# Turning the keys of a gated-recurrence layer by DMA and ScalarE instead of by TensorE

## The chip, the cores and the metric

The kernel runs on one core of one Trainium2 chip. The metric is the device time of one execution in microseconds, the median over the runs shown. The engines are TensorE (PE, its weight loads PEld), VectorE (DVE), ScalarE (ACT), GpSimd (POOL), and SyncE (SP), whose queue issues nearly all transfers of this kernel. Each engine works through its own instructions in order.

## The reference, cut to what matters

One layer over 2048 latent tokens and 256 context tokens of width 1024: adaLN-modulated norm, one input projection to 9216 columns, two groups of heads, one output projection, gated residual, final norm. Eight heads of width 128 run a gated linear recurrence in both directions; a gated short convolution fills the other half.

```python
def chunk_scan(q, k, v, logf, s0):
    """S_t = diag(f_t) S_{t-1} + k_t v_t^T, o_t = S_t^T q_t, chunkwise."""
    def step(S, inp):
        qc, kc, vc, gc = inp
        bcum = jnp.cumsum(gc, axis=2)
        ...
        o = einsum('bhts,bhsv->bhtv', attn, vc) + einsum('bhtk,bhkv->bhtv', qc * jnp.exp(bcum), S)
        S_new = jnp.exp(b_last)[..., None] * S + einsum(
            'bhsk,bhsv->bhkv', kc * jnp.exp(b_last[:, :, None, :] - bcum), vc)
        return S_new, o
...
q, i, zf, zb = [p_hg[..., j * HG_WIDTH:(j + 1) * HG_WIDTH] for j in range(4)]
f_f = lb_f + (1.0 - lb_f) * sigmoid(zf)      # k = 1 - f, logf = log(f); the same backward
o, _, _ = bidir_scan(q, kf, kb, v, gf, gb, s_f, s_b)     # s_f, s_b: states after the context
y_hg = hgrn_out(o, p[..., 4 * HG_WIDTH:HG_COLS], hg_onorm_w[l], x.dtype)
```

## The kernel before, in words

**Stretches.** The program is written as 50 stretches (`stretch`, from line 1255 on): 32 head stretches (head `a` of 8, i = 0 to 3, each one segment of 512 tokens), four of the first convolution block, 14 pairs, and then the output projection. A head runs its four segments forward if its number is even, backward if odd (`prim`). So the group of tokens changes at i = 1, 2 and 3, and stays the same from i = 3 to the next head's i = 0.

**Products.** A head stretch has two units (gates, then values and queries), a third one for the output gates at odd i, and at i = 0 three short ones for the context. A unit is the seven products of a Strassen-like scheme (`seven`, line 954), each 4 x 3 matmuls of 128x128 by 128x256 f16, as each operand is split into a high and a low half. ScalarE copies out the banks `p1`, `p5` and `u2` (`keep`, line 970) before the next product adds onto the same bank, and VectorE takes the four results (`plus`, line 974). The last product of a unit is issued after the first product of the next (`finish_unit`). The right-hand operands ("hop" tiles, nine, seven to a stretch) are loaded by SyncE at line 1423 as the last unit of the stretch before frees them.

**The order of the work.** Everything else is cut into steps with a weight (`PACE`, `paced`): `chain` (the scan) and `extra` (second passes, gates, w_out). `merge_steps` spreads each list over the stretch by its weights, and `run` issues a step when its share of the ticks is reached; a tick is three matmuls, 28 to a unit. What is left is issued at the end of the stretch. So a step's place in every engine's queue, SyncE's too, is written by hand through its weight. The weights of the scan's steps (the context's first step, `c_first`, has 1.5; `out2` 1.0, `rstd` 0.63):

```python
PACE = {
...
        "c_levels": 4.27, "c_keys": 0.85, "c_states": 0.31, "values": 0.65, "begin": 1.0, "levels": 1.55, "held": 1.1,
        "level6": 2.64, "keys": 1.0, "states": 2.0, "out": 0.53, "states2": 1.14,
...
```

**The scan of a segment** runs in the stretch after its own (`scan_steps`): the values are turned, then levels 0 to 6 multiply the keys K and queries Q by gate products (`levels`, `held`, `level6`, `update`; VectorE at L509, L516, L522, ScalarE's mixed copies at L626, TensorE's attention blocks A at L656, L675, L682 into the pool `pa`). The gates' products are written into a tile `tot` of their own. Then the keys are turned, then the chunk states are formed, then the output:

- `key_turn` (line 692): for each of the two directions four TensorE transposes of 128x128 f32 into a bank of `px` (L697), and one copy out by ScalarE (L699).
- `states`: four products T of turned keys and values per direction (`outer`, L706); VectorE steps the states of the head's own direction (L750); ScalarE keeps the other direction's T (`Ts`, L755).
- `outp`: eight products o (L762, L763) and a copy by ScalarE (L765).

**Segments with fast values.** From segment 7 on (`FAST = 7`, to segment 31) the values are turned without TensorE, by `Turn`: `over` reads the 128x512 f32 tile as 128x1024 two-byte words in one transposing DMA (L122), `back` brings the halves into place with four DMAs (L128), and `join` interleaves them into f32 by a ScalarE copy (L132). Segments 0 to 6 use `value_turn`: four TensorE transposes and a copy.

**Second passes.** When a head's four segments are done, the other direction runs over them (`second_steps`: VectorE steps states Z at L802, four products at L809, an addition at L810, four sums of squares by ScalarE at L812); then `head_rstd` (twelve small VectorE operations, L155 to L161) and `y_steps` (scaling by ScalarE at L858, four transposes at L864, VectorE at L866). All four second passes of a head and its rstd stand in the i = 1 stretch of the next head; `y_steps` follow in i = 2, i = 3 and i = 0.

**Buffers.** PSUM has eight banks: three for the products (`pm`), three in `pa`, two in `px` (turned values and keys, T, o, second passes, turned outputs, weight scales). The tag `pair` of the pool `hp` has four tiles of 2 KB a partition; it holds a transfer turn's two tiles, the early stores, and in heads 6 and 7 the rows of w_out that `wo_scan` loads and sums. K and f have two tiles each, Q six, the `ring` ten.

Of the kernel before, what the change touches and what calls it, by code (L numbers as in the profile page):

```python
# [33 lines left out]
FAST = 7  # L34
# [28 lines left out]
def hybrid_layer(ctx: ExitStack, tc, x, cx, w_ada, b_ada, w_in, w_out, fnorm_w, small_d, masks, ident_d, sel_d, out):  # L63
# [15 lines left out]
    pa = ctx.enter_context(tc.tile_pool(name="pa", bufs=3, space=PSUM))  # L79
    px = ctx.enter_context(tc.tile_pool(name="px", bufs=2, space=PSUM))  # L80
# [33 lines left out]
    class Turn:  # L114
# [5 lines left out]
        def over(s):  # L120
            s.a = hp.tile([P, 2 * NCH, P], U16, tag="pair", name=f"ta_{s.nm}", bufs=4)
            SY.dma_start_transpose(s.a, s.src().bitcast(U16))  # L122

        def back(s):
            s.b = hp.tile([P, NCH, 2, P], U16, tag="pair", name=f"tb_{s.nm}", bufs=4)
            for h in range(2):
                for b in range(2):
                    SY.dma_start(s.b[64 * b:64 * b + 64, :, h, :], s.a[h::2, b::2, :])  # L128
# [136 lines left out]
    def norm_group(ntile, src, row0, m, nm, first_ops=None, space=q_tile):  # L265
# [72 lines left out]
        def store2(ops, k, row, eng):  # L338

            n2 = len(ops)  # L340
            pair = hp.tile([P, n2, 2, HW], F16, tag="pair", name=f"hp{ops[0]}_{nm}{k}", bufs=4)
# [189 lines left out]
    class Seg:  # L531
# [208 lines left out]
    def scan_steps(h, s):  # L740
# [26 lines left out]
        turn_v = Turn(lambda: s.vT, f"v{s.nm}")  # L767

        def joined():
            s.v = turn_v.join()  # L770

        over, back, join = [], [], []
        if s.fast:
            over, back, join = [paced(0.2, turn_v.over)], [paced(0.2, turn_v.back)], [paced(0.6, joined)]
        return (over + ([] if s.fast else [paced("values", s.value_turn)]) + [paced("begin", s.begin_levels)]
                + [paced("levels", lambda: s.levels(0))] + back + [paced("held", lambda: s.held(1)),
                   paced("levels", lambda: s.levels(2)), paced("held", lambda: s.held(3))] + join
                + [paced("levels", lambda: s.levels(4))]
                + [paced("held", lambda: s.held(5)), paced("level6", s.level6), paced("keys", s.key_turn), paced("states", states),
                   paced("out", outp)])  # L780
# [266 lines left out]
    def wo_scan(k):  # L1047
        for j in range(2):
            half = hp.tile([P, GW], F32, tag="pair", name=f"wos{k}{j}", bufs=4)
            SY.dma_start(half, w_out[0, k * P:(k + 1) * P, j * GW:(j + 1) * GW])  # L1050
            S.activation(junk[:, :GW], half, AF.Abs, accum_out=late.rs[:, 2 * k + j:2 * k + j + 1])
# [179 lines left out]
    for hd in range(HEADS):  # L1231
# [29 lines left out]
    for wi, (kind, a, i) in enumerate(stretch):  # L1261
        units, chain, extra = [], [], []
        if kind == "head":
# [26 lines left out]
            if i == 1:  # L1290
                chain += context_steps(h)
# [7 lines left out]
        if wi > 0 and stretch[wi - 1][0] == "head":  # L1299
            _, pa_h, pi = stretch[wi - 1]  # L1300
            chain += scan_steps(heads[pa_h], heads[pa_h].segs[pi])
# [5 lines left out]
        if prev is not None:  # L1307
            if i == 1:
                for j in range(NG):
                    extra += second_steps(prev, j)  # L1310
# [4 lines left out]
            elif i == 2 and prev is tail:  # L1315
# [403 lines left out]
```

## Time and profile before

| | |
|---|---|
| median of three runs | 2147.5 us (2145.26 to 2148.08) |
| profiled execution | 2148.78 us, span 2147.0 us |
| TensorE busy | 2065.5 us (96%) |
| VectorE busy | 1648.6 us (77%) |
| ScalarE busy | 1203.0 us (56%) |
| GpSimd busy | 193.8 us (9%) |
| DMA queue q1, share of 16 engines | 47.0% |
| granted TensorE clock | 0.994 |

The span is from the first to the last instruction of the profiled execution; the time of an execution is somewhat longer than its span. Busy time is the union of an engine's instructions. TensorE's matmuls overlap: a matmul's duration is its latency, and what it occupies is the distance to the next one's start. In a row of the timeline the columns are start, duration, engine, line, operation, output and inputs, and count; rows with "q" behind the engine are its sequencer's or its DMA issues. A tile's row gives the shortest, median and longest duration in ns and the first and last start in us. A row of waits gives the waiting instruction, whom it waited for, total us, times and the longest.

### The profile page before, as it was taken

How to read it: one execution, taken by the hardware profiler on the slowest of the kernel's cores; microseconds unless marked ns; L12 is line 12 of the kernel's file. 1: busy time of each engine (PE TensorE's matmuls, PEld its weight loads, DVE VectorE, ACT ScalarE, POOL GpSimd, SP SyncE). 2: the span in 40 equal slices, each digit the busy share in tenths (PEclk: the TensorE clock that was granted, in tenths of full speed). 3: DMA queues.
4: the chain of work that ended last, by engine and by line, in shares of the span. 5: the costliest groups of instructions: out<-in, count | busy, mean ns of one | idle time of the engine just before them, and what ended most of it. 6: DMA issues, size and time to landing. Idle time of an engine off the chain costs nothing. (4 is left out here: it accounts for less than half of the span.)

```text
span 2147.0 us, 53020 instructions
## 1 busy us (share of the span) xinstructions
PE 2065.5 (96%) x22011; PEld 1455.3 (68%) x22011; DVE 1648.6 (77%) x3413; ACT 1203.0 (56%) x2406; POOL 193.8 (9%) x272
## 2 busy tenths in 40 slices
PE   5988999999999999999999999999999999999998
PEld 2877878888888888888888887444444444444443
DVE  6787988878778787788787877687778655687775
ACT  7965666767567666676776655345444423333332
POOL 0121111111111111111111100000000000000000
PEclk8999999999999999999999999999999999999999
DMA  9567533452445343544654568833443105542421
GB/s 357 192 209 265 180 120 128 146 173 86 135 137 159 116 133 119 180 114 153 193 168 131 152 198 254 255 125 101 138 138 99 62 28 189 198 144 89 136 80 59
DMA packets 239398, 324.12 MB, mean 151 GB/s; under 512 B 66611, under 2 KB 168371, under 8 KB 237365
## 3 DMA queue, kind: packets, MB, share of 16 engines
q1 hardware_dynamic: 236996, 316.80, 47.0%
q8 instruction: 172, 2.82, 0.5%
q10 hardware_dynamic: 2160, 3.93, 0.5%
q14 instruction: 70, 0.57, 0.1%
HBM read 240.19 MB, written 67.37 MB: 143 GB/s over the span
## 5 line engine op out<-in xcount | busy, mean ns | idle before, releaser
L964 PEld LDWEIGHTS <-e_p 128*128 128x128 f16 x1332 | 130.4, 98 | 68.7 <-issue 19.0
L509 DVE TENSOR_TENSOR K<-K,tot 128x512 f32<-128x512 f32 x192 | 135.6, 706 | 42.8 <-ACT km L626 25.9
L626 ACT ACTIVATE km<-K 128x512 f32<-128x512 f32 x192 | 129.2, 674 | 69.7 <-DVE K L509 65.5
L963 PEld LDWEIGHTS <-e_p 128*128 128x128 f16 x1332 | 130.4, 98 | 53.2 <-issue 1.4
L965 PEld LDWEIGHTS <-e_p 128*128 128x128 f16 x1332 | 130.4, 98 | 52.0 <-issue 0.9
L516 DVE TENSOR_TENSOR Q<-Q,tot 128x512 f32<-128x512 f32 x192 | 132.9, 692 | 26.5 <-PE A L656 15.1
L633 POOL COPY qm<-Q 128x512 f32<-128x512 f32 x96 | 80.7, 840 | 781.6 <-DVE Q L516 781.6
L964 PEld LDWEIGHTS <-whib_p 128*128 128x128 f16 x888 | 87.0, 98 | 38.6 <-issue 5.2
L963 PEld LDWEIGHTS <-whib_p 128*128 128x128 f16 x888 | 86.9, 98 | 37.2 <-issue 0.8
L963 PEld LDWEIGHTS <-whia_p 128*128 128x128 f16 x888 | 86.9, 98 | 35.9 <-DMA hop3B<-Hd3B 2.4
L965 PEld LDWEIGHTS <-wloa_p 128*128 128x128 f16 x888 | 86.8, 98 | 35.1 <-issue 1.3
L965 PEld LDWEIGHTS <-wlob_p 128*128 128x128 f16 x888 | 86.9, 98 | 34.4
L964 PEld LDWEIGHTS <-whia_p 128*128 128x128 f16 x888 | 86.9, 98 | 33.4 <-issue 1.3
L181 ACT ACTIVATE e_p<-ws_p,sc_p 128x512 f16<-128x512 f32 x108 | 77.2, 718 | 56.9 <-DVE ws_p L468 40.0
L690 POOL COPY A<-Ac 32x128 f32<-32x128 f32 x128 | 79.5, 621 | 132.9 <-ACT A L686 103.8
L886 ACT ACTIVATE cv<-c,small 128x512 f32<-128x512 f32 (+1 forms) x36 | 24.3, 674 | 112.5 <-DVE c L904 63.3
L970 ACT ACTIVATE u<-sa,sx_w 128x256 f32<-128x256 f32 (+1 forms) x111 | 58.1, 523 | 47.0 <-PE sa L965 38.2
L1630 POOL TENSOR_TENSOR x_o<-x_o,fw 128x512 f32<-128x512 f32 x1 | 1.3, 1266 | 871.0 <-ACT junk L1621 871.0
L182 DVE SCALAR_TENSOR_TENSOR e_p<-ws_p,sc_p,e_p 128x512 f16<-128x512 f32 x108 | 79.4, 747 | 0.0
L433 ACT ACTIVATE junk<-ws_p 128x1024 f16<-128x1024 f32 x72 | 75.6, 1050 | 5.1 <-DMA ws_p<-in_w_in 4.9
L181 ACT ACTIVATE hiS_o<-y_o,sc_y 128x1024 f16<-128x1024 f32 x32 | 36.7, 1148 | 72.9 <-PE sa_o L964 32.1
L970 ACT ACTIVATE p<-sa,sx_w 128x256 f32<-128x256 f32 (+1 forms) x111 | 57.4, 517 | 24.1 <-PE sa L965 24.1
(863 smaller groups left out, 7044.8 us busy)
## 6 DMA issues: line engine op xcount, KB each, us to landing
ws_p<-in_w_in SPq DMA_DIRECT2D x72, 512.0 KB, 4.4
y_o<-yT SPq DMA_DIRECT2D x32, 512.0 KB, 4.2
xt_x<-in_x SPq DMA_DIRECT2D x16, 512.0 KB, 6.0
wa<-in_w_ada SPq DMA_DIRECT2D x16, 512.0 KB, 10.1
Gd<-zs SPq DMA_DIRECT2D x32, 256.0 KB, 2.9
sg<-Gd SPq DMA_DIRECT2D x32, 256.0 KB, 3.7
yT<-y SPq DMA_DIRECT2D x32, 256.0 KB, 2.4
wos<-in_w_out SPq DMA_DIRECT2D x32, 256.0 KB, 3.3
```

Source lines behind the costliest of these rows:

```text
L181: S.activation(hi, src, AF.Copy, scale=st[:, 0:1])
L182: V.scalar_tensor_tensor(lo, src, st[:, 0:1], hi, ALU.mult, ALU.subtract)
L433: S.activation(junk.rearrange("p (k n) -> p k n", k=KT), stage[i], AF.Abs, accum_out=r)
L509: V.tensor_tensor(m, m, sub(cur, nb + 1, [[2, np_], [-(nb + 1), 2], [0, B]]), ALU.mult)
L516: V.tensor_tensor(m, m, sub(cur, 1, [[2, np_], [nb - 1, 2], [0, B]]), ALU.mult)
L626: S.activation(sub(s.km, 0, [[2 * B, n // (2 * B)], [B, 2], [1, B]]), mix(s.K, n, B, n // (2 * B)), AF.Copy)
L633: G.tensor_copy(sub(qm, 0, [[2 * B, n // (2 * B)], [B, 2], [1, B]]), mix(s.qf, n, B, n // (2 * B)))
L690: G.tensor_copy(A3[js, :, js], s.Ac[js])
L963: PE.matmul(ps, hi[:, k], rh, start=start and k == 0, stop=False, skip_group_check=not start)
L964: PE.matmul(ps, hi[:, k], right(name, 1, k), start=False, stop=False, skip_group_check=not start)
L965: PE.matmul(ps, lo[:, k], rh, start=False, stop=k == nk - 1, skip_group_check=not start)
L970: last_keep.append(S.activation(r, ps, AF.Copy, scale=sx))
```

## The change

For segments 7 to 30 (`FAST = (7, 31)`), the keys too go through `Turn`, one turn for each direction. Segment 31 goes back to the TensorE turn for values, and keeps it for the keys. The steps of two segments now share a stretch (`scan_chain`): the new segment's levels, and the old segment's key joins, states and output, which are so issued about half a stretch later than before. The keys' transfers are the last step of the chain. The totals are written over the gates (`s.tot = s.f`). `pa` goes from three banks to two, `px` from two to three, the tag `pair` from four tiles to six. For heads whose last segment is fast, two of the second passes stay in the next head's i = 1 stretch, behind a pause of weight 8, and the other two and the rstd go to i = 2. `wo_scan` is split into a step that fetches and a step that sums.

```diff
-FAST = 7
+FAST = (7, 31)
-    pa = ctx.enter_context(tc.tile_pool(name="pa", bufs=3, space=PSUM))
-    px = ctx.enter_context(tc.tile_pool(name="px", bufs=2, space=PSUM))
+    pa = ctx.enter_context(tc.tile_pool(name="pa", bufs=2, space=PSUM))
+    px = ctx.enter_context(tc.tile_pool(name="px", bufs=3, space=PSUM))
...
-            s.tot = ring(f"tot_{s.nm}") if s.small else scp.tile([P, 2 * GW], F32, tag="tot", name=f"tot_{s.nm}",
-                                                                 bufs=1)
+            s.tot = ring(f"tot_{s.nm}") if s.small else s.f
...
+    def scan_chain(old, new, context):
+
+        a = scan_steps(heads[new.hd], new) if new else {}
+        b = scan_steps(heads[old.hd], old) if old else {}
+        steps = []
+        add = lambda w_, fn: steps.append(paced(w_, fn))
+
+        def old_keys():
+            old.kT = {i: old.turns[i].join() for i in old.sides}
+
+        if new is None or not new.fast:
+            if old:
+                add(1.0, old_keys)
+                add("states", b["states"])
+                add("out", b["out"])
+            steps += context
+            for k in SCAN if new else ():
+                add(KIND.get(k, k), a[k])
+            return steps
+        prim = heads[new.hd].prim
+        new.sides = (prim, 1 - prim)
+        new.turns = [Turn(lambda i=i: new.K[:, i * new.n:(i + 1) * new.n], f"k{new.nm}{i}") for i in range(2)]
+        turn_v = Turn(lambda: new.vT, f"v{new.nm}")
...
+        def keys():
+            for i in new.sides:
+                new.turns[i].over()
+            for i in new.sides:
+                new.turns[i].back()
+
+        add(0.2, turn_v.over)
+        add("begin", a["begin"])
+        steps += context[:2]
+        if old and context:
+            add(0.6, old_keys)
+        steps += context[2:]
+        add("levels", a["l0"])
+        if old and context:
+            add("states", b["states"])
+            add("out", b["out"])
+        add(0.0, turn_v.back)
+        add("held", a["h1"])
+        add("levels", a["l2"])
+        add("held", a["h3"])
+        if old and not context:
+            add(0.6, old_keys)
+        add("levels", a["l4"])
+        if old and not context:
+            add("states", b["states"])
+        add("held", a["h5"])
+        if old and not context:
+            add("out", b["out"])
+        add(0.6, value)
+        add("level6", a["level6"])
+        add(0.6, keys)
+        return steps
...
-            s.fast = hd * NG + i >= FAST
+            s.fast = FAST[0] <= hd * NG + i < FAST[1]
...
-            if i == 1:
-                for j in range(NG):
+            late_ = prev.segs[-1].fast
+            if i == 1 and late_:
+                extra += [paced(8.0, lambda: None)] + second_steps(prev, 0) + second_steps(prev, 1)
+            elif i == (2 if late_ else 1):
+                for j in range(2 if late_ else 0, NG):
                     extra += second_steps(prev, j)
                 extra.append(paced("rstd", lambda prev=prev: head_rstd(prev)))
...
-            extra += [paced(0.2, lambda k=k: wo_scan(k)) for k in (2 * n, 2 * n + 1)]
+            extra += wo_scan(2 * n) + wo_scan(2 * n + 1)
```

More of the change, by code (lines that the diff above doesn't have):

```diff
@@ L120, in over @@
         def over(s):
-            s.a = hp.tile([P, 2 * NCH, P], U16, tag="pair", name=f"ta_{s.nm}", bufs=4)
+            s.a = hp.tile([P, 2 * NCH, P], U16, tag="pair", name=f"ta_{s.nm}", bufs=6)
             SY.dma_start_transpose(s.a, s.src().bitcast(U16))
         def back(s):
-            s.b = hp.tile([P, NCH, 2, P], U16, tag="pair", name=f"tb_{s.nm}", bufs=4)
+            s.b = hp.tile([P, NCH, 2, P], U16, tag="pair", name=f"tb_{s.nm}", bufs=6)
             for h in range(2):
@@ L340, in store2 @@
             n2 = len(ops)
-            pair = hp.tile([P, n2, 2, HW], F16, tag="pair", name=f"hp{ops[0]}_{nm}{k}", bufs=4)
+            pair = hp.tile([P, n2, 2, HW], F16, tag="pair", name=f"hp{ops[0]}_{nm}{k}", bufs=6)
             hi, lo = pair[:, :, 0], pair[:, :, 1]
@@ L765, in outp @@
             S.activation(s.o, po, AF.Copy)
[L767 to L780, printed above, removed]
+        return {"values": s.value_turn, "begin": s.begin_levels, "l0": lambda: s.levels(0), "h1": lambda: s.held(1),
+                "l2": lambda: s.levels(2), "h3": lambda: s.held(3), "l4": lambda: s.levels(4), "h5": lambda: s.held(5),
+                "level6": s.level6, "keys": s.key_turn, "states": states, "out": outp}
@@ new lines, in hybrid_layer, with value @@
+    SCAN = ("values", "begin", "l0", "h1", "l2", "h3", "l4", "h5", "level6", "keys", "states", "out")
+    KIND = {"l0": "levels", "l2": "levels", "l4": "levels", "h1": "held", "h3": "held", "h5": "held"}
+    def scan_chain(old, new, context):
[18 more added lines that the diff above has]
+        turn_v = Turn(lambda: new.vT, f"v{new.nm}")
+        def value():
+            new.v = turn_v.join()
+        def keys():
[29 more added lines that the diff above has]
+        return steps
@@ L1047, in wo_scan, with fetch, sums @@
     def wo_scan(k):
[L1048 to L1051, printed above, removed]
+        half = []
+        def fetch():
+            for j in range(2):
+                half.append(hp.tile([P, GW], F32, tag="pair", name=f"wos{k}{j}", bufs=6))
+                SY.dma_start(half[j], w_out[0, k * P:(k + 1) * P, j * GW:(j + 1) * GW])
+        def sums():
+            for j in range(2):
+                S.activation(junk[:, :GW], half[j], AF.Abs, accum_out=late.rs[:, 2 * k + j:2 * k + j + 1])
+        return [paced(0.8, fetch), paced(0.2, sums)]
     def wo_scale():
@@ L1289, in hybrid_layer @@
                     units.append(gate_unit(h, g))
-            if i == 1:
-                chain += context_steps(h)
         else:
@@ L1298, in hybrid_layer @@
         group_of.append(g if kind != "pair" else None)
-        if wi > 0 and stretch[wi - 1][0] == "head":
-            _, pa_h, pi = stretch[wi - 1]
-            chain += scan_steps(heads[pa_h], heads[pa_h].segs[pi])
+        new, old = [heads[stretch[k][1]].segs[stretch[k][2]] if k >= 0 and stretch[k][0] == "head" else None
+                    for k in (wi - 1, wi - 2)]
+        old = old if old and old.fast else None
+        chain += scan_chain(old, new, context_steps(heads[a]) if kind == "head" and i == 1 else [])
         prev = None
@@ L1307, in hybrid_layer @@
         if prev is not None:
-            if i == 1:
-                for j in range(NG):
+            late_ = prev.segs[-1].fast
[3 more added lines that the diff above has]
+                for j in range(2 if late_ else 0, NG):
                     extra += second_steps(prev, j)
@@ L1314, in hybrid_layer @@
                     extra += tail_y[0][:1] + tail_y[1][:1]
-            elif i == 2 and prev is tail:
+            if i == 2 and prev is tail:
                 extra += tail_y[0][1:] + tail_y[1][1:] + tail_y[2][:1] + tail_y[3][:1]
```

## The prediction

> **What bounds the kernel now.** First the page's head, then busy time by stretch (columns: window, its length, busy time and count by engine, granted clock, DMA share, GB/s).
>
> ```profile
> span 2147.0 us, 53020 instructions
> ...
> PE 2065.5 (96%) x22011; PEld 1455.3 (68%) x22011; DVE 1648.6 (77%) x3413; ACT 1203.0 (56%) x2406; POOL 193.8 (9%) x272
> ```
> ```profile
> 356.00:1260.00 904.00, 882.70 (x13510) 778.15 (x13508) 729.50 (x1603) 609.30 (x1355) 126.56 (x179) 1.00 0.49 143
> 267.20:299.90 32.70, 31.59 (x505) 27.89 (x504) 28.84 (x76) 20.28 (x65) 4.56 (x8) 1.00 0.36 114
> 551.20:591.60 40.40, 40.13 (x584) 35.62 (x582) 30.91 (x82) 23.28 (x70) 5.30 (x7) 1.00 0.31 88
> 591.60:618.70 27.10, 27.10 (x470) 23.98 (x469) 19.60 (x39) 19.19 (x43) 4.14 (x7) 1.00 0.61 184
> 618.70:695.60 76.90, 74.13 (x1114) 64.89 (x1113) 65.58 (x133) 53.97 (x101) 10.89 (x14) 1.00 0.49 132
> ```
>
> The first window is the part the key turn is taken from: TensorE (PE) works 882.7 of 904 us at full granted clock, and VectorE (DVE) 81%. The other four are stretches of a head, bounded by the first product on a new hop tile: i=1, i=1, i=2, and i=3 with the next i=0. The short stretch (i=2, 27.1 us) is pure TensorE, idle nowhere, with VectorE at 72% and ScalarE (ACT) at 71%. So a TensorE instruction taken out is worth its full issue time, as long as nothing else takes its place.
>
> ```profile
> PE sa L963 <- ACT u L970: 6.9, 10, 1.1
> ...
> PE T L706 <- ACT kT L699: 1.8, 4, 0.8
> ...
> PE T L706 <- DVE y L866: 1.3, 4, 0.3
> PE kT L697 <- DVE Q L810: 1.0, 4, 0.2
> ...
> PE ss_p L169 <- ACT Ts L755: 0.9, 1, 0.9
> ```
>
> These are TensorE's waits in the same 904 us (total, times, longest): all are small. The last four hang on the key turn or on the two banks of px. `u` shows the weak point: a product that accumulates onto a bank must wait until ScalarE has copied the bank out.
>
> **The change, part by part.** *Key turns off TensorE.* One turn of both sides:
>
> ```profile
> 610.56 0.27 PE L965 MATMUL sc<-hop14B,wloa_p 128*128 128x256 f16 x1
> 610.67 1.04 PE L697 MATMUL kT<-ident,K 128*128 128x128 f32 x8
> 611.54 0.27 PE L963 MATMUL sc<-hop14B,whia_p 128*128 128x256 f16 x1
> ```
> ```profile
> L697 PE MATMUL kT<-ident,K x256: 272/273/328, 126.0 to 1257.7; 128*128 128x128 f32 x128
> ...
> L699 ACT ACTIVATE kT<-kT x64: 574/593/618, 127.6 to 1258.1; 128x512 f32<-128x512 f32 x64
> ```
>
> An ordinary product follows the last one after 0.11 us; behind the eight transposes it starts at 611.54 instead of 610.67. So a turn holds up the stream by 0.87 us, and 24 segments (7 to 30) give 24 x 0.87 = 20.9 us. Segment 31 gets its values turned by TensorE again: four transposes, half of 0.87, +0.4. [...]
>
> *Waits that go.* Keys leave px and the T products no longer stand right behind the copies: the four waits above (1.8 + 1.3 + 1.0 + 0.9 = 5.0) can go, of which I take 3 (bounds 0 and 5), as second passes still use px.
>
> *ScalarE's joins.*
>
> ```profile
> L132 ACT ACTIVATE t_v<-tb_v x25: 1155/1167/1186, 375.5 to 1247.8; 128x1024 uint16<-128x1024 uint16 x25
> ```
> ```profile
> L970 ACT ACTIVATE u<-sa,sx_w x111: 449/474/689, 144.1 to 1835.9; 128x256 f32<-128x256 f32 x83, 128x512 f32<-128x512 f32 x28
> ```
>
> Two joins of 1.167 replace two copies of 0.593: +1.15 us a segment, 27.6 in all, on an engine busy 609 of 904 us. They are hidden except where a `p1` or `u2` copy is queued behind: its bank is wanted again after one product, 12 x 0.109 = 1.31 us, less the copy's 0.47, so 0.84 us of slack. The joins stand in a row, 2.33 us; a copy due in the first 1.49 us is late by 0.75 on average. A unit of 28 ticks has two such copies in 28 x 0.48 = 13.5 us (27.10 us over 56 ticks), so 2 x 1.49/13.5 x 0.75 = 0.17 us a segment, 4.0 in all (bounds 0 and 24 x 1.49 = 36; I take 4.0, near the lower one, since `u` costs only 6.9 today).
>
> *SyncE's queue and the transfers.*
>
> ```profile
> L122 SPq DMA_TRANSPOSE ta_v<-vT x25: 1267/1273/1607, 356.7 to 1230.1; - x25
> ...
> DMA to landing us min/median/max: 3.1/3.9/6.1
> ```
> ```profile
> L128 SPq DMA_DIRECT2D tb_v<-ta_v x100: 594/616/1817, 363.2 to 1237.0; - x100
> ...
> DMA to landing us min/median/max: 2.1/2.3/6.7
> ```
> ```profile
> 434.03 1.27 SPq L122 DMA_TRANSPOSE ta_v<-vT  x1
> 435.39 0.53 SPq L1423 DMA_DIRECT2D hop10T<-Hd2T  x1
> 437.18 2.98 SPq L128 DMA_DIRECT2D tb_v<-ta_v  x4
> ```
>
> The keys' step issues two transposes and eight moves, and the queue waits in between for the first to land. By medians: transposes issued at 0 and 1.27, landed at 3.9 and 5.2; eight moves at 0.66 each until 9.2; the last landed at 11.5 us. Queued behind are this stretch's last two hop loads (needed a stretch later), then the next stretch's value transposes, gate loads and stage loads. The keys start at weight 15.52 of 16.12, tick 50 of 52; the join comes at 6.5 of 16.12 of the next stretch. With an i=2 stretch next, that is 2 + 4 + 21 = 27 ticks, 13.1 us; with i=1 (6.97 of 23.05 of 80 ticks) 14.5; with i=3 or i=0 18. So the transfers are just in time and I cost them at nothing; the cover is 1.6 us in the tightest stretch, and a first landing of 6.1 instead of 3.9 uses it up. The next gates write K some 30 ticks after its transposes, 14 us against 5.2: no wait. Totals in f: f is written again only two stretches on, nothing.
>
> *Second passes move.* For heads 1 to 6, two of four second passes and the rstd go from the next head's i=1 stretch to its i=2 stretch.
>
> ```profile
> L802 DVE SCALAR_TENSOR_TENSOR Z<-Z,tot,Ts x112: 318/350/829, 275.4 to 1274.4; 128x128 f32<-128x128 f32 x112
> ```
> ```profile
> L810 DVE TENSOR_TENSOR Q<-Q,o x32: 672/680/689, 279.8 to 1284.2; 128x512 f32<-128x512 f32 x32
> ```
> ```profile
> L161 DVE SCALAR_TENSOR_TENSOR rsy_o<-rsa_o,rsy_o x24: 167/174/177, 300.0 to 1290.3; 128x16 f32<-128x16 f32 x24
> ```
> ```profile
> L812 ACT ACTIVATE junk<-Q x128: 292/309/313, 280.5 to 1286.3; 128x128 f16<-128x128 f32 x128
> L812 ACT ACTIVATION_READ_ACCUMULATOR junk<-Q x128: 185/187/202, 280.7 to 1286.5; 128x1 f32 x128
> ```
>
> VectorE there gets 8 x 0.35 + 2 x 0.68 + 12 x 0.17 = 6.2 us on top of 19.60, ScalarE 8 x 0.50 + 1.15 = 5.1 on top of 19.19. The shortened stretch of 26.2 us then holds 25.8 of VectorE and 24.3 of ScalarE: nearly three full engines. At 88% VectorE (window 267.20) TensorE idled 1.11 us, at 85% (window 618.70) 2.77 of 76.9. For 98% I take 1.0 us a stretch, six stretches, 6 (bounds 0 and 2.5 each, 15). The i=1 stretch, relieved, has only 0.27 us of idle to give back.
>
> *Two banks for pa, three for px.* In the first three stretches a turn of x fills two pa banks.
>
> ```profile
> L320 ACT ACTIVATE h_x<-xT_x,ab x24: 760/770/792, 65.8 to 169.9; 128x512 f32<-128x512 f32 x24
> ```
>
> With two banks, one of these copies may stand ahead of a scan product: 12 turns x 0.77 = 9.2 at most, 0 at least; the turns stand some 4 us apart, so 1. The w_out fetch and its sums, parted, cost nothing: the sums move away from the load.
>
> Sum: -20.9 + 0.4 - 3.0 + 4.0 + 1.0 + 6.0 = -12.5 us. The profiled execution took 2148.8 (span 2147.0 and 1.8 around it), 1.3 above the median of the three runs; from the median 2147.5 that gives 2135.0.
>
> **The rivals.**
>
> *Keys come late (slower).* Place: the join in the i=1 and i=2 stretches. If the transfers slip past 13 us, ScalarE, which works in order, stands at the join with `u2` and `p1` behind it.
>
> ```profile
> ACT t_v L132 <- DMA tb_v<-ta_v: 9.6, 3, 3.6
> ```
>
> Such waits exist already: three, 3.2 us on average. 3.2 - 0.84 = 2.4 us lost in each of the 12 segments with a tight stretch after them is +28: 2135 + 28 = 2163. It decides from a landing 0.84 + 1.1 us past the join on every second segment (12 x 1.1 = 13 eats the gain). For it: 1.6 us of cover, three transposes a stretch where there was one, and DMA already at 61% of its share in the short stretch. Against: only 3 of 25 value joins waited. [...] Chance 0.15.
>
> *The short stretch becomes VectorE's and ScalarE's (no change).* If 98% costs the full 2.5 us in six stretches and the joins cost 8 instead of 4: -12.5 + 9 + 4 = 0.5, about 2148. For it: the sums above; against: i=3 runs at 85% with little idle. Chance 0.13.
>
> *Occupancy is the 273 ns (much faster).* 192 x 0.273 = 52.4 saved: some 2104. The 0.87 us gap speaks against it. Chance 0.02.
>
> **How the numbers follow.** My forecast, 0.70, is 2135; its own range runs from 2119 (-20.5 with all 5 us of waits back and the stalls near nothing) to 2145. The other bounds and most of the second rival reach 2150; the slower rival lies above. About 0.2% (4.3 us) is what a measurement of this kernel can tell from no change. Faster by more: 0.67 of the forecast, 0.02 of the third, 0.01 of the second: 0.70. Same: 0.03 + 0.11 = 0.14. Slower: 0.15 + 0.01 = 0.16.
>
> **What would show it.** Right: kT transposes drop from 256 to 64, TensorE's busy time by about 20 us, the waits T on kT gone; 72 joins of 1.17 us; the last move of a key landed before its join; short stretches of 26 to 28 us with VectorE above 90%. Wrong: ScalarE waiting for tb_k for over 1 us in most stretches with TensorE behind `u`, short stretches longer than 28 us, or a TensorE that is busy less and idle as much more.

## The result and the profile after

The changed kernel takes 2193.97 us (median of four runs, 2192.15 to 2200.1) against 2146.5 us for the kernel before on the same chip: a ratio of 1.0226, 95% interval 1.0204 to 1.0247. That is 47 us slower where 12.5 us faster was forecast. The profiled execution took 2200.1 us.

The head of the page after, with busy time and count by engine:

```profile
span 2198.0 us, 53097 instructions
...
PE 2070.6 (94%) x21823; PEld 1449.0 (66%) x21823; DVE 1644.8 (75%) x3413; ACT 1239.0 (56%) x2406; POOL 184.1 (8%) x272
```

TensorE has 188 matmul records fewer than before (192 transposes of keys fewer, and four more for the values of segment 31), yet it is busy 5 us longer and the span is 51 us longer. The counts by line say that the change did what it says: 64 transposes for keys are left of 256, and ScalarE does 72 joins of 1.16 us. (From here on line numbers differ by some lines from kernel to kernel: `km` is L626 before and L625 after.)

```profile
L696 PE MATMUL kT<-ident,K x64: 272/273/329, 133.9 to 1313.8; 128*128 128x128 f32 x64
```
```profile
L132 ACT ACTIVATE t_k<-tb_k x48: 1154/1165/1181, 427.3 to 1292.0; 128x1024 uint16<-128x1024 uint16 x48
L132 ACT ACTIVATE t_v<-tb_v x24: 1157/1162/1175, 407.1 to 1275.9; 128x1024 uint16<-128x1024 uint16 x24
```

By stretch (columns as in the prediction; the first row is the part with transferred keys, the others are i=1, i=2, and i=3 with the next i=0, of the head whose stretches the prediction quotes):

```profile
371.20:1315.00 943.80, 882.45 (x13316) 769.70 (x13314) 726.41 (x1601) 643.18 (x1355) 113.32 (x178) 0.97 0.65 163
564.70:605.50 40.80, 38.52 (x561) 34.20 (x559) 28.57 (x72) 21.94 (x49) 5.46 (x7) 0.96 0.50 95
605.50:636.80 31.30, 29.53 (x478) 25.73 (x476) 20.98 (x53) 24.05 (x64) 4.03 (x7) 0.95 0.75 200
636.80:713.00 76.20, 72.20 (x1097) 62.92 (x1095) 68.88 (x138) 56.07 (x101) 8.03 (x14) 1.00 0.68 168
```

The short stretch is 31.3 us instead of 27.1, and TensorE, which never stood there, now idles 1.8 us of it; its granted clock is 0.95 and not 1.00. The i=1 stretch won nothing (40.8 against 40.4). TensorE's largest waits in the same part, and two of ScalarE's:

```profile
PE A L655 <- ACT km L625: 19.7, 13, 4.3
PE T_c L705 <- ACT kT_c L698: 11.6, 6, 2.3
PE sa L1014 <- DVE f L1025: 7.7, 5, 5.4
PE sa L1014 <- ACT u L1021: 7.4, 10, 1.7
```
```profile
ACT km L625 <- DVE K L509: 55.5, 55, 5.0
ACT t_k L132 <- DMA tb_k<-ta_k: 40.2, 19, 4.9
```

The two largest waits of TensorE were under 1 us each before: the attention blocks A wait for `km`, and the context's T_c (its products of turned keys and values) for its turned keys. Both are copies by ScalarE that can stand behind a join in its queue. Of ScalarE's two waits the first is no larger than before (55.0 us), the second is new. One such chain, from the time lines of SyncE, ScalarE and TensorE (start, length, and in brackets the idle time before, with what ended it):

```profile
458.43 6.40 SPq L128 DMA_DIRECT2D tb_k<-ta_k  x8
467.34 2.10 SPq L122 DMA_TRANSPOSE ta_v<-vT  x1
```
```profile
466.26 1.17 ACT L132 ACTIVATE t_k<-tb_k 128x1024 uint16<-128x1024 uint16 x1 [3.79 <-DMA tb_k<-ta_k]
467.33 0.61 ACT L625 ACTIVATE km<-K 128x512 f32<-128x512 f32 x1
```
```profile
468.00 0.46 PE L655 MATMUL A<-Q,km 128*32 128x32 f32 x32 [3.13 <-ACT km L625]
```

ScalarE stands 3.79 us at a join whose moves have not landed, the copy `km` queued behind it is late, and TensorE stands 3.13 us. And that is not the end of it: two windows of granted clock (the third figure from the end), right behind this gap and behind one for T_c that ended at 578.21.

```profile
469.30:472.70 3.40, 3.40 (x19) 2.42 (x17) 2.75 (x9) 2.42 (x7) 1.15 (x1) 0.50 1.06 330
578.50:581.90 3.40, 3.40 (x62) 2.80 (x62) 1.69 (x4) 1.11 (x4) 0.00 (x0) 0.50 0.10 24
```

For 3.4 us after the gap TensorE runs at half speed, busy all the time. Between 330 and 1380 us the records of the clock show 12 such pieces, 51 us long together, so up to 25.5 us (an estimate: half of the 51) are lost that no view of waits shows; in the kernel before there is none. That is enough to explain why TensorE is busy 5 us longer with some 20 us less of work.

### The profile page after: what moved, and what is told of

Same layout as the page of the kernel before. It is cut to its first block, busy times and chain, and to the rows that moved or that the text cites. A ratio compares the mean times of both kernels' runs of the same rounds, so it can differ in the third digit from the quotient of the medians.

```text
span 2198.0 us, 53097 instructions
## 1 busy us (share of the span) xinstructions
PE 2070.6 (94%) x21823; PEld 1449.0 (66%) x21823; DVE 1644.8 (75%) x3413; ACT 1239.0 (56%) x2406; POOL 184.1 (8%) x272
## 5 line engine op out<-in xcount | busy, mean ns | idle before, releaser
L509 DVE TENSOR_TENSOR K<-K,f 128x512 f32<-128x512 f32 x224 | 176.2, 787 | 44.9 <-PE A L681 27.5
L516 DVE TENSOR_TENSOR Q<-Q,f 128x512 f32<-128x512 f32 x224 | 166.5, 744 | 19.7 <-PE A L655 17.7
L625 ACT ACTIVATE km<-K 128x512 f32<-128x512 f32 x192 | 129.2, 674 | 91.1 <-DVE K L509 78.5
L1015 PEld LDWEIGHTS <-e_p 128*128 128x128 f16 x1332 | 131.7, 99 | 64.3 <-issue 13.4
L632 POOL COPY qm<-Q 128x512 f32<-128x512 f32 x96 | 91.8, 957 | 686.1 <-DVE Q L516 681.2
L1016 PEld LDWEIGHTS <-wlob_p 128*128 128x128 f16 x888 | 88.0, 99 | 35.5
L1021 ACT ACTIVATE u<-sa,sx_w 128x256 f32<-128x256 f32 (+1 forms) x111 | 57.9, 521 | 46.1 <-PE sa L1016 38.7
L689 POOL COPY A<-Ac 32x128 f32<-32x128 f32 x128 | 55.6, 435 | 292.1 <-ACT A L685 235.1
L132 ACT ACTIVATE t_k<-tb_k 128x1024 uint16<-128x1024 uint16 x48 | 55.9, 1167 | 40.4 <-DMA tb_k<-ta_k 40.2
```

The costliest lines, as they stand in the source:

```text
L132: S.activation(r.bitcast(U16).rearrange("p (c d h) -> p c d h", c=NCH, h=2), s.b.rearrange("p c h d -> p c d h"), AF.Copy)
L509: V.tensor_tensor(m, m, sub(cur, nb + 1, [[2, np_], [-(nb + 1), 2], [0, B]]), ALU.mult)
L516: V.tensor_tensor(m, m, sub(cur, 1, [[2, np_], [nb - 1, 2], [0, B]]), ALU.mult)
L625: S.activation(sub(s.km, 0, [[2 * B, n // (2 * B)], [B, 2], [1, B]]), mix(s.K, n, B, n // (2 * B)), AF.Copy)
L632: G.tensor_copy(sub(qm, 0, [[2 * B, n // (2 * B)], [B, 2], [1, B]]), mix(s.qf, n, B, n // (2 * B)))
L1015: PE.matmul(ps, hi[:, k], right(name, 1, k), start=False, stop=False, skip_group_check=not start)
```

## The experiments

Eighteen kernels were run. Each ratio is to runs of the kernel before on the same chip (medians from 2144.6 to 2147.7 us). The intervals of the ratios are 0.1 to 0.3% wide to either side, so a price that is a difference of two medians carries 2 to 6 us of uncertainty.

**Single parts, added to the kernel before.** First the second passes and the rstd of heads 1 to 6, moved as the change moves them:

```diff
-            if i == 1:
-                for j in range(NG):
+            late_ = 1 <= prev.hd <= 6
+            if i == 1 and late_:
+                extra += [paced(8.0, lambda: None)] + second_steps(prev, 0) + second_steps(prev, 1)
+            elif i == (2 if late_ else 1):
+                for j in range(2 if late_ else 0, NG):
```

> The kernel before with one part of the change alone: for heads 1 to 6, two of the four second passes and the rstd go from i=1 to i=2. Theory A: within 4 us of the kernel before (2142 to 2151). Theory B: 20 us or more above it, with the short stretch going from 27.1 to over 30 us. My prediction's own step had 6 us for it.

Measured: 2148.41 us, ratio 1.0012 (1.0002 to 1.0021): +2.5 us. The i=2 stretches grew from 27.1 to 28.7 us with TensorE idle nowhere: the passes brought their own products with them, and the i=1 stretch shrank in turn (40.4 to 38.7).

The banks alone (`pa` 3 to 2, `px` 2 to 3):

```diff
-    pa = ctx.enter_context(tc.tile_pool(name="pa", bufs=3, space=PSUM))
-    px = ctx.enter_context(tc.tile_pool(name="px", bufs=2, space=PSUM))
+    pa = ctx.enter_context(tc.tile_pool(name="pa", bufs=2, space=PSUM))
+    px = ctx.enter_context(tc.tile_pool(name="px", bufs=3, space=PSUM))
```

> The kernel before with the banks alone: two for pa, three for px. In the changed kernel and in the run without key turns the first product of stretch 7 starts 12 to 13 us later than before, ahead of any key that a transfer turns. Theory D (turned x and the scan's A blocks wait for each other's two pa banks): stretch 7 starts 6 to 13 us later than 331.9, total 2150 to 2160. Rival: banks cost nothing, the totals written over the gates do; then 2143 to 2148 here and the loss in the next run. My prediction had 1 us for the banks.

Measured: 2146.77 us, ratio 1.0009 (0.9997 to 1.0021). No difference from none.

The totals over the gates alone:

```diff
-            s.tot = ring(f"tot_{s.nm}") if s.small else scp.tile([P, 2 * GW], F32, tag="tot", name=f"tot_{s.nm}",
-                                                                 bufs=1)
+            s.tot = ring(f"tot_{s.nm}") if s.small else s.f
```

> The kernel before with the totals alone written over the gates. Theory D: within 3 us of the kernel before. Rival (the gates' tile is held until level 6, so the gates after next wait for it): stretch 7 starts 6 to 13 us later, total 2150 or more.

Measured: 2181.15 us, ratio 1.0159 (1.0128 to 1.0189): +36 us, with no key turned otherwise than before. One line of the change, the one that was costed at nothing, loses more than the whole change was to win. The time lines show why. Before, around one segment's first levels:

```profile
587.75 0.69 DVE L509 TENSOR_TENSOR K<-K,tot 128x512 f32<-128x512 f32 x1
594.96 0.56 PE L656 MATMUL A<-Q,km 128*32 128x32 f32 x32
595.55 1.12 DVE L516 TENSOR_TENSOR Q<-Q,f 128x512 f32<-128x512 f32 x1 [1.11 <-PE A L656]
```

With the totals in f, the same place:

```profile
611.60 0.56 PE L655 MATMUL A<-Q,km 128*32 128x32 f32 x32
613.49 1.10 DVE L516 TENSOR_TENSOR Q<-Q,f 128x512 f32<-128x512 f32 x1
614.63 0.68 DVE L522 TENSOR_TENSOR f<-f 128x512 f32<-128x512 f32 x1
615.35 1.03 DVE L509 TENSOR_TENSOR K<-K,f 128x512 f32<-128x512 f32 x1
616.41 0.63 ACT L625 ACTIVATE km<-K 128x512 f32<-128x512 f32 x1 [1.33 <-DVE K L509]
617.13 0.46 PE L655 MATMUL A<-Q,km 128*32 128x32 f32 x32 [0.79 <-ACT km L625]
```

In both, the first product of Q with the gates (L516) overwrites Q and must wait until TensorE's first block has read it. Before, VectorE had by then already made the totals and the K of a later level (587.75), since `tot` was another tile. Now the total overwrites f, which that same Q still has to read; so total, K, `km` and the next A run one after the other behind TensorE. ScalarE's waits of `km` for K are 114.8 us in this run, 65.5 before.

**Parts taken out of the changed kernel.** No key transfers and no joins; the turned values stand in for turned keys:

```diff
-            old.kT = {i: old.turns[i].join() for i in old.sides}
+            old.kT = {i: old.v for i in old.sides}
...
-            for i in new.sides:
-                new.turns[i].over()
-            for i in new.sides:
-                new.turns[i].back()
+            pass
```

> The key turn of segments 7 to 30 is left out altogether, no transfers and no joins; the turned values stand in for the turned keys. It is the bound of what taking the key turn off TensorE can bring. Theory A and theory C: 2118 to 2130 (20 us of TensorE gone, some waits too). Theory B: 2150 or more, since the second passes are where the change put them.

Measured: 2149.68 us, ratio 1.0013 (1.0004 to 1.0023): even with the key turn removed at no cost, nothing is won.

The transfers made, but no join (only the first of these two edits):

> The changed kernel with the keys' transposes and moves, but without their joins; the turned values stand in for the turned keys. It parts the 24 us between the run without a key turn (2149.7) and the run whose joins read a scratch tile (2173.5). Theory H (ScalarE's 27 us more of joins, in the way of p and u copies): 2148 to 2156. Rival I (the transfers themselves: SyncE's queue and the DMA engines, hop and weight loads late): 2165 to 2175.

Measured: 2175.31 us, ratio 1.0135 (1.0115 to 1.0155). So transfers that nobody waits for cost 25.6 us.

Transfers and joins, but the joins read a scratch tile of ScalarE and so wait for no transfer:

```diff
             r = ring(f"t_{s.nm}")
+            if s.nm[0] == "k":
+                S.activation(r.bitcast(U16).rearrange("p (c d h) -> p c d h", c=NCH, h=2),
+                             junk.bitcast(U16).rearrange("p (c h d) -> p c d h", c=NCH, h=2), AF.Copy)
+                return r
```

> The key joins read a scratch tile that only ScalarE writes instead of the transferred keys; transposes, moves and joins are all still made, so the turned keys are meaningless and only the wait for the transfer is gone. Theory A: 2125 to 2145, no wait of ScalarE before a key join, TensorE's wait for kT_c (12.7 us) below 5. Theory B: 2180 or more. Theory C: 2180 or more, since the joins and the transfers are still there.

Measured: 2173.52 us, ratio 1.0127 (1.0112 to 1.0142). The joins' own 2 x 1.17 us cost nothing that shows beside the run before (2175.31); the waits for transferred keys cost 2193.97 - 2173.52 = 20 us.

**Where the joins stand.** Held behind the `km` copies that the text of the program lists ahead of them:

```diff
+            def joins():
+                for i in old.sides:
+                    old.kT[i] = old.turns[i].join()
+            follow(km_marks, joins)
```

> The key joins are held behind the scan's mixed copies that the program writes ahead of them; nothing else changes. Theory A (a join stands in ScalarE's queue ahead of copies that the scan needs sooner, and waits there for its transfer): ScalarE's wait for tb_k falls from 40 us to under 20, TensorE's wait for km from 21 us to under 8, the half-clock stretches between 400 and 1300 us from twelve to six or fewer, time 2150 to 2170 (the i=1 stretches, whose joins stand ahead of the context's key copies, stay as they are). Theory B (the moved second passes overfill the short stretch) and theory C (the joins' own length and the transfers' traffic load ScalarE and the queues): 2185 to 2195, as the load is the same.

Measured: 2189.89 us, ratio 1.0196 (1.0179 to 1.0213), 4 us of the 20. TensorE's wait for `km` fell from 19.7 to 6.5 us, but its wait for `u` copies rose from 7.4 to 13.8 us, and that of T_c stayed (10.4 us).

In the i=1 stretches, the context's steps ahead of the key joins, and the joins held behind the context's key copies in ScalarE's queue:

```diff
-        steps += context[:2]
+        steps += context
+        add("levels", a["l0"])
         if old and context:
             add(0.6, old_keys)
-        steps += context[2:]
-        add("levels", a["l0"])
-        if old and context:
             add("states", b["states"])
```

> The changed kernel, with the i=1 stretches alone altered: the old segment's joins come after the context's keys and states and the first level, and are held behind the context's key copies in ScalarE's queue. Theory F (in i=1 the context's key copies stand behind joins that wait for their transfers, and TensorE's T_c behind the copies): TensorE's wait for kT_c falls from 12.7 us to under 4, the i=1 stretches of heads 2 to 7 from 40.1 us on average to about 38, time 2176 to 2184. Rival G (the waits only move to the next copy in line): 2190 or more.

Measured: 2179.77 us, ratio 1.0158 (1.0138 to 1.0179): 14 us won. TensorE's wait for the context's keys is

```profile
PE T_c L706 <- ACT kT_c L699: 2.8, 6, 0.5
```

instead of 11.6: part of the 20 us was the copy `kT_c` queued behind joins that waited.

**Totals of levels 0 and 1 in a tile of their own** (3 KB, with five `pair` tiles instead of six so that it fits):

```diff
-            s.tot = ring(f"tot_{s.nm}") if s.small else s.f
+            s.tot = ring(f"tot_{s.nm}") if s.small else scp.tile([P, GW + HW], F32, tag="tot", name=f"tot_{s.nm}",
+                                                                 bufs=1)
...
+            if lev == 2:
+                s.tot, s.off = s.f, 0
```

> The changed kernel with the totals of levels 0 and 1 in a tile of their own again, as before (the later ones still over the gates); it has room for five pair tiles instead of six. Theory J (the totals written over the gates must wait until the queries of level 0 have read the gates, and those wait for TensorE's first A block; so the keys and their mixed copies of the next levels, which ran ahead of TensorE before, run behind it): VectorE's K of levels 1 to 3 ahead of the first A block again, TensorE's wait for km from 21 us to under 10, time 2160 to 2175. Rival K (in the changed kernel the wait for the keys' transfers sets the pace and hides it): 2185 or more.

Measured: 2171.56 us, ratio 1.0128 (1.0108 to 1.0149): 22.4 us back. Nine of them come ahead of any transferred key: the first product of stretch 7 starts at 335.8 us instead of 345.1 (331.9 in the kernel before). The granted clock of the profiled execution rises from 0.981 to 0.990, and of TensorE's 19.7 us of waiting for `km` next to nothing is left, though the joins still stand where they stood:

```profile
PE A L658 <- ACT km L626: 0.4, 1, 0.4
```

The same with the context first:

> The run before it, and in the i=1 stretches the context's steps ahead of the joins as well. If the two costs add up: 14 us below the run before it, 2146 to 2161. If they hide each other: within 5 us of it.

Measured: 2162.35 us, ratio 1.0084 (1.0069 to 1.0099).

The bound: the totals of all levels in a tile of their own (with four `pair` tiles), no key transfers, no joins (values stand in for the turned keys):

> The changed kernel without any key turn (turned values stand in for turned keys), with the totals in their own tile as before: banks, second passes and late states are as changed. It is the bound that 20.5 us less of TensorE would have given. Theory J: 2122 to 2134, 16 to 28 us below the same run with the totals over the gates (2149.7). Rival K or a loss from the late states: 2140 or more.

Measured: 2133.46 us, ratio 0.9950 (0.9935 to 0.9965), 11.6 us faster than the kernel before. TensorE's busy time falls from 2065.5 to 2041.4 us, so the work taken off TensorE is about as large as forecast; how much of it comes out as time is taken up below.

**Why the transfers cost 25 us.** Own totals for levels 0 and 1, transfers, no joins:

> Totals in their own tile; the keys' transposes and moves are issued as in the changed kernel, but no join reads them: the values stand in for the turned keys. The run with neither transfers nor joins and own totals gave 2133.5 us. Theory: the transfers cost about 25 us by themselves, as they did with totals over the gates: 2155 to 2161. Rival: that cost came about only because TensorE was already waiting behind the totals: 2133 to 2142.

Measured: 2159.17 us, ratio 1.0069 (1.0054 to 1.0084): +25.7 on the bound, as on the other base. All of it lies in the short stretches (27.7 us there in the bound for four heads, 31.6 to 32.7 here; 30.9 against 35.5 and 38.0 for the two heads that fetch w_out). One such stretch in the bound, then in this run:

```profile
585.00:612.70 27.70, 27.70 (x478) 24.82 (x476) 20.89 (x56) 22.41 (x65) 3.58 (x7) 1.00 0.51 167
```
```profile
588.10:620.10 32.00, 28.55 (x478) 24.95 (x477) 21.97 (x57) 20.88 (x61) 2.50 (x5) 1.00 0.88 204
```

The two runs also differ in the totals of the higher levels (over the gates here) and in the `pair` tiles (five here, four in the bound).

The moves reading the identity matrix, so that SyncE does not wait for the transposes' landing; the traffic stays:

```diff
+                    src = s.a[h::2, b::2, :]
+                    if s.nm[0] == "k":
+                        src = sub(ident[h::2].bitcast(U16), b * P, [[0, NCH], [1, P]])
-                    SY.dma_start(s.b[64 * b:64 * b + 64, :, h, :], s.a[h::2, b::2, :])
+                    SY.dma_start(s.b[64 * b:64 * b + 64, :, h, :], src)
```

> As the run before it, but the eight key moves read the identity matrix instead of the transposed keys, so that SyncE need not wait for the landing of the two key transposes before it issues them; the number and the size of the transfers stay as they are (the moved data means nothing and is not used). Theory of the queue (SyncE stands at the moves, and what is queued behind is late): most of the cost goes, 2134 to 2144. Rival, the traffic itself (short packets on the DMA engines slow the others): as the run before it, within 4 us.

Measured: 2156.62 us, ratio 1.0054 (1.0039 to 1.0069). Only 2.6 us less, which the uncertainty covers, so SyncE's wait for the landing is not it, and the rival (the traffic) seemed to stand. But the time lines of the run before it, at its short stretch from 446.3 us on, point to something else:

```profile
434.18 0.47 DVE L1028 SCALAR_TENSOR_TENSOR vT<-sb,sx_w,u 128x256 f32<-128x256 f32 x1
```
```profile
444.41 2.16 SPq L122 DMA_TRANSPOSE ta_k<-K  x1
...
449.21 6.14 SPq L128 DMA_DIRECT2D tb_k<-ta_k  x8
...
457.91 2.45 SPq L122 DMA_TRANSPOSE ta_v<-vT  x1
465.10 2.60 SPq L128 DMA_DIRECT2D tb_v<-ta_v  x4
```
```profile
469.41 1.17 ACT L132 ACTIVATE t_v<-tb_v 128x1024 uint16<-128x1024 uint16 x1 [3.72 <-DMA tb_v<-ta_v]
```

The *values* are ready at 434.65 and SyncE gets to them at 457.91: they are queued behind the keys of the segment before, and ScalarE stands 3.72 us at the value join, with gate copies and `u` behind it. In the kernel before, the corresponding value transpose (quoted in the prediction, 434.03) was issued the moment the values were ready. The profile after has the same: `ta_v` at 467.34, in the fence above, 22 us after its values.

The joins of the other stretches held back too (on the run with own totals and context first):

```diff
-            follow(kc_marks if context else [], joins)
+            follow(kc_marks if context else km_marks, joins)
```

> The changed kernel with level 0 and 1 totals in a tile of their own, the context's steps ahead of the key joins in the i=1 stretches, and in all other stretches the key joins held in ScalarE's queue behind the km copies that the text lists ahead of them. The run without this last hold gave 2162.4 us. Theory: the joins that ScalarE still waits for (28.2 us in 11 waits there) are those of the i=2 stretches, and held back they are covered: 2152 to 2158. Rival: what the hold saves comes back as later u copies, as in the run of the changed kernel with joins held, which won 4: 2160 to 2164.

Measured: 2168.80 us, ratio 1.0120 (1.0103 to 1.0137), 6 us worse. The waits of joins for keys fell from 28.2 to 5.4 us and bought nothing: the short stretches stayed at 31 to 35 us. That the late values hold them there is an argument at this point; the last run tests it.

The key moves issued from GpSimd's queue:

```diff
-                    SY.dma_start(s.b[64 * b:64 * b + 64, :, h, :], s.a[h::2, b::2, :])
+                    (G if s.nm[0] == "k" else SY).dma_start(s.b[64 * b:64 * b + 64, :, h, :], s.a[h::2, b::2, :])
```

> As the first run of this call, but the key moves are issued from GpSimd's queue, which is 8% busy, and not from SyncE's. Theory of the queue: SyncE goes on to the value transposes and the loads, and 10 to 20 us are won: 2136 to 2146. Rival of the traffic: no change, 2152 to 2158. Second rival: GpSimd issues slowly and stands at the landings itself, and the context's and the short queries' work that it does for TensorE (qm) comes late: over 2160.

Measured: 2292.36 us, ratio 1.0688 (1.0661 to 1.0714). The second rival held: TensorE's blocks wait for GpSimd's copies of Q, which stand behind the moves (ahead of moves GpSimd stood 64.3 us until a key's transpose had landed, at most 8.0 us at a time, and 164.0 us with no wait that the profile shows).

```profile
PE A L661 <- POOL qm L636: 95.7, 15, 11.4
```

The values ahead of the previous segment's keys, everywhere:

```diff
         add(0.2, turn_v.over)
+        add(0.0, turn_v.back)
+        if old:
+            add(0.6, lambda: keys(old))
         add("begin", a["begin"])
...
-        add(0.6, keys)
+        if last:
+            add(0.6, lambda: keys(new))
```

> As the run with own totals and key transfers that no join reads (2159.2 us; 2133.5 without the transfers), but on SyncE's queue a segment's value transposes and value moves stand ahead of the previous segment's key transposes and key moves, and not behind them; the number of transfers is the same. Theory: the 25 us are the values, which are ready 10 to 24 us before SyncE gets to them, so that ScalarE stands at the value join of every i=2 stretch: 2134 to 2142, i=2 stretches 28 us again. Rival: the issue time and the traffic of the transfers cost it in any order: 2154 to 2160.

Measured: 2165.86 us, ratio 1.0096 (1.0067 to 1.0126): no better (6.7 us more, which the spread of these runs, 2160.4 to 2173.6, does not tell from none), and yet the short stretches are cured. Windows of one i=2 and one i=1 stretch:

```profile
588.90:616.90 28.00, 28.00 (x478) 24.98 (x477) 21.43 (x57) 22.59 (x65) 3.87 (x9) 1.00 0.75 212
698.30:741.30 43.00, 38.63 (x560) 33.83 (x558) 30.08 (x72) 19.67 (x44) 3.48 (x7) 0.96 0.54 132
```

The i=2 stretches are 27.8 to 29.1 us, the i=1 stretches 38.7 to 43.0 instead of 37.4. Ahead of the i=1 and i=3 stretches the key transposes now start 10 to 15 us later than in the run with keys first, and a new wait appears: the next gates are to overwrite the K that a late transpose still reads.

```profile
ACT K L549 <- DMA ta_k<-K: 11.8, 7, 3.3
```

In the second window above, the context's `kT_c` stands behind that wait in ScalarE's queue, and TensorE behind `kT_c`:

```profile
713.29 0.63 ACT L549 ACTIVATE K<-f 128x512 f32<-128x512 f32 x1 [3.30 <-DMA ta_k<-K]
```
```profile
714.25 1.41 PE L708 MATMUL T_c<-v_c,kT_c 128*128 128x128 f32 x8 [4.04 <-ACT kT_c L701]
```

The whole computation in this order (own totals, context first):

> The whole computation: own totals, the context's steps ahead of the key joins in the i=1 stretches (2162.4 us so far), and the values ahead of the keys on SyncE's queue as in the run before. Theory: most of the 25 us of the transfers goes here too, 2138 to 2148. Rival: the keys, now behind the values, land later and the key joins in the i=2 stretches wait for them: 2152 to 2162.

Measured: 2190.92 us, ratio 1.0222 (1.0191 to 1.0253). The wait of the gates for late transposes is there too (8.0 us), but the rival is larger: the keys land later, ScalarE waits for them in 28 joins (35.6 us), and TensorE's products T stand behind joins.

```profile
PE T L709 <- ACT t_k L132: 21.8, 14, 4.3
```

Last, the values first ahead of the i=2 stretches alone. In heads 2 to 5 the keys' first transpose there starts 2.3 us ahead of the stretch, 1.9 in the run with keys first; in heads 6 and 7, which fetch w_out, it comes 7.6 and 8.0 us later than in that run:

```diff
+        place = heads[new.hd].segs.index(new)
         add(0.2, turn_v.over)
+        if place == 1:
+            add(0.0, turn_v.back)
+            add(0.6, lambda: keys(old))
...
-        add(0.6, keys)
+        if place:
+            add(0.6, lambda: keys(new))
```

> As the run with own totals and key transfers that no join reads (2159.2 us; 2133.5 without the transfers), with the values ahead of the previous segment's keys on SyncE's queue in one place only: ahead of each i=2 stretch, where the keys' transposes start within 2 us of where they did. In the other three places of a head the order stays. Theory: late values at the six i=2 stretches are the cost of the transfers, and the loss of the run with values first everywhere came from keys moved back by 12 to 14 us in the other places: 2132 to 2142, i=2 stretches 28 to 29 us (31 to 38 before) and i=1 stretches 37.5. Rival: the time goes to another wait however the queue is ordered: 2150 to 2160.

Measured: 2133.49 us, ratio 0.9929 (0.9910 to 0.9949): by the medians the whole 25.7 us are back, with every transfer still made. SyncE's rows for the values of the segment shown above, and the windows of an i=1 and an i=2 stretch of the next head:

```profile
435.10 1.27 SPq L122 DMA_TRANSPOSE ta_v<-vT  x1
...
438.19 2.60 SPq L128 DMA_DIRECT2D tb_v<-ta_v  x4
```
```profile
547.70:585.00 37.30, 37.05 (x561) 33.12 (x559) 28.50 (x70) 19.15 (x43) 3.53 (x6) 1.00 0.53 131
585.00:613.00 28.00, 27.99 (x479) 24.98 (x477) 21.02 (x56) 22.62 (x65) 3.39 (x8) 1.00 0.72 193
```

So the order on one in-order queue, at one place of a head, is worth about as much as the transfers had cost, and traffic, landing and issue time together leave no cost that the medians show. They may still cost something in the heads that fetch w_out: in this profile (2139.4 us, the slowest of the four executions) the three i=3 stretches from head 5 on, each with the one behind it, are 13.6 us longer together than in the bound, while what lies between the start of stretch 7 and them is 6 us shorter. One of them in the bound, then in this run:

```profile
1036.90:1113.20 76.30, 72.25 (x1097) 63.02 (x1096) 60.25 (x122) 52.08 (x105) 9.73 (x16) 1.00 0.57 158
```
```profile
1035.80:1118.00 82.20, 75.51 (x1097) 64.94 (x1095) 60.43 (x122) 53.78 (x111) 9.79 (x15) 0.96 0.71 178
```

## Why the prediction was wrong, step by step

The runs form a ladder from the bound to the changed kernel, each step a difference of two medians: 2133.5 (bound); +25.7 for the transfers in the order of the change; +3.2, within the uncertainty, for the joins and their waits, context first (to 2162.4); +9.2 for joins ahead of the context's steps (2171.6); +22.4 for the totals over the gates (2194.0).

- **"Totals in f: f is written again only two stretches on, nothing."** This step failed worst: 22.4 us in the changed kernel, 36 alone. The prediction looked for the next *writer of f by the gates* and not for the remaining *readers of f* when the total is written over it. The price of the missing tile is the run-ahead that it had given VectorE. (In the changed kernel that run-ahead was also the slack of `km`: with it, the wait for `km` behind joins is 0.4 us, without it 19.7.)
- **"The transfers are just in time and I cost them at nothing."** Half right. The last run shows no cost of the transfers as such, within its uncertainty and with the heads that fetch w_out left open. But their place had one: the prediction itself lists "the next stretch's value transposes" as queued behind the keys, and priced only the keys' own landing. The values had no join to miss in its sum, although three of their joins waited even before. 25.7 us.
- **The cover of the keys, 13.1 us.** The rival "keys come late" named the wait and its place rightly, at 0.15, though not all that it held up; its price of +28 stands against 20 us measured, or 9.2 + 3.2 where the totals are out of the way. The cover was computed from the weights, in the belief, which the part of this document ahead of the prediction states too, that weights fix each engine's queue. They do not: the built kernel's queue of ScalarE has a join ahead of `km` copies that the program lists first. In the i=1 and i=2 stretches ScalarE came to the first join 7.5 to 10.6 us after the keys' first transpose, not 13.1 to 14.5, and the keys that this join reads landed 10.8 to 12.9 us after it. So the landing (11.5 forecast) was nearly right, and the cover was wrong.
- **What is queued behind a join.** Only `p1` and `u2` were priced (4.0). The joins' own length costs nothing measurable, but `km` (19.7) and `kT_c` (11.6) were not in the list.
- **The clock.** The sum takes full clock throughout. With stalls of 1.5 to 5.4 us came 51 us at 0.50 in the changed kernel, by the estimate above up to 25.5 us of its time; the bound ran at a granted clock of 1.00 from 340 to 1260 us. This is contained in the steps of the ladder and does not come on top.
- **Key turns, -20.9, and waits that go, -3.** Right in TensorE's work, which falls by 24 us from before to the bound (2065.5 to 2041.4). In time, with second passes and banks at their measured 2.5 and about 2, the bound's -11.6 leaves -16 where these terms and the values of segment 31 make -23.5; the other 7 us were not separated by a run. The traces place them at the heads that fetch w_out: against the run with moved second passes, the bound's i=2 stretches there take 30.9 us instead of 29.4 and 29.9, and head 7's i=3 stretch with the one behind it 72.1 instead of 67.5. The cause stays open.
- **Second passes, +6.0.** Too dear: 2.5 us. VectorE is at 74% in that stretch, not 98%; part of the moved work ran in the end of the stretch before.
- **Banks, +1.0.** Within what was measured.
- **The range.** Its lower end, 2119, does not follow from its own terms: -20.5 and all 5 us of waits from 2147.5 give 2122.
- **The sign.** Each of the two missed terms alone is larger than the whole expected gain.

Open: the last run's order was not tried with the joins in place, and the last run does not compute the layer, as the values stand in for the keys. From the ladder, that order with the joins would take 2133.5 + 3.2, some 2137 us; but with values first everywhere the short stretches with joins were up to 5.5 us longer than without (the two of the heads that fetch w_out the most), so the joins' waits, hidden so far behind the late values, may come out. That the whole change can beat the kernel before is thus argued and not shown.

## What to carry to other kernels

Writing a result over an operand to save a buffer is not free because the operand's buffer is free later: list every reader still to come, and what each of them waits for, as the writer and all that follows it inherits that wait (36 us for the totals alone). When transfers are added to an in-order queue, price what was behind them on the queue and not only their own landing; here the cure was an exchange of neighbours in one place (25.7 us), and moving them everywhere held another buffer too long (11.8 us of the gates' waits for late transposes). A stall of TensorE of 1.77 us here was followed by 3.4 us at a granted clock of 0.50, so compare the clock's windows as well as the waits.

## What the runs showed of the hardware

The half clock came with short gaps of TensorE. In the changed kernel a gap of 1.77 us that ended at 615.12 was followed by 3.4 us at 0.50 from 616.1 on, and one of 2.28 us by the window of 578.50 above, while gaps of 1.70 and 2.04 us (ended at 683.8 and 726.3) were followed by none. The twelve pieces between 330 and 1380 us are 3.4 or 6.8 us long. So the length of a gap alone does not tell here whether half clock follows it; what decides was not shown.

With the key moves on GpSimd's queue nothing was won: SyncE was spared the issue of 192 moves, and the kernel was 124 us slower (2292.4 against 2168.8), as GpSimd's own copies came late (95.7 us of TensorE's waits for `qm`). The order within one engine's queue is another matter: the same transfers, exchanged with their neighbours, were worth 25.7 us.
